# The second layer's gate projections by seven block products for eight, and an attention table in a buffer of its own

## Chip, cores and metric

The kernel runs on one core of one Trainium2 chip. The metric is the time of one execution in device microseconds, the median of several runs.

## The reference

Two layers of a trunk over 1024 latent tokens and 256 context tokens, width 1024, float32. In each layer four token mixers (chunked gMLP, Fourier, convolution, neighbourhood attention) give branch rows a, b, cc, d of width 256, which are merged through gates:

```python
za, zb, zcv, zq, zk, zv, zg = jnp.split(h @ w_in[l], SPLITS, axis=-1)
...
def merge_branches(a, b, cc, d, zg, w_a, w_b, w_c, w_d, w_o):
    ga, gb, gc, gd = jnp.split(jax.nn.sigmoid(zg), N_BRANCH, axis=-1)
    m = ga * (a @ w_a) + gb * (b @ w_b) + gc * (cc @ w_c) + gd * (d @ w_d)
    return m @ w_o
```

zg, the gate projection, is 1024 tokens by 4 x 1024 columns. A mixture of experts follows the merge. In the second layer context tokens are needed only as keys and values, so that its gates cover the 1024 latent tokens alone.

## The kernel before

Every operand of a large matmul is kept as two parts. `split` makes them: ACT copies the operand to a float32r tile (hi, L422), and DVE subtracts that from the operand (lo, L423). `mm3` (L427 to L429) multiplies hi by hi, hi by lo and lo by hi into one PSUM sum: three matmuls for one k-tile of 128, each with a moving operand of 512 tokens.

`gates` (L1092) runs once for each layer, transposed: output columns on partitions, tokens along the row. Its loops are over four branches i and, inside, eight column blocks d of 128. For each (i, d), `proj_T` multiplies the weight block by the tokens' normed rows (tiles hTh and hTl, eight k-tiles, two halves of 512 tokens): 48 matmuls into one PSUM tile A of 128x1024. ACT takes the sigmoid from A into g (L1158). Then 12 matmuls multiply the branch rows (bh, bl, two k-tiles) by the branch weights (wbh, wbl) into another A, and DVE multiplies that by g and adds it to mT (L1173, or L1175 and L1176), which holds all of m in SBUF.

Weights come by SP's queue through the class `Split`, which splits them in order and ahead. Branch rows are stored in DRAM (`self.br`) and loaded by POOL's queue in `load` (L1132), twice for each branch, when the branch changes; ACT and DVE split them.

PSUM tiles come from pools that hand out tile A (1024 wide, two banks) and X and T (512 wide). SBUF tiles come from pools with a number of buffers for each name; a new tile of a name waits for the last use of the one whose place it takes. Each engine runs its instructions in the order of the program.

`merge_out` (L1194) multiplies m by w_out, token tile by token tile. While the first weights are split, eight plain matmuls (L1219) of the first k-tile from mT fill TensorE; `out_m` (L1354) splits m for a token tile. POOL's queue loads the router's weights (L1206), the norm's gains and rows of modulation (L1340) at its start.

In the attention, POOL makes a bias table `Bu` of a unit's kind (L282) that DVE adds to the scores (L317, the start of the softmax); two pairs of `Bu` buffers alternate, both taken from the pool that is opened for the attention. `Vw` holds windows of the values, loaded by 16 DMAs on SP's queue (L264).

Of the kernel before, what the change touches and what calls it, by code (L numbers as in the profile page):

```python
# [18 lines left out]
D = 1024  # L19
SEQ = 1024  # L20
CTX = 256
# [3 lines left out]
KD = D // 128  # L25
# [77 lines left out]
class Split:  # L103
# [62 lines left out]
    def ready(self, n):  # L166

        self.prefetch()
        self.split(self.i + n)
# [13 lines left out]
class Attention:  # L183
# [10 lines left out]
    def __init__(self, K, p, V, Vc):  # L194
        self.K, self.V, self.Vc, self.nc = K, V, Vc, K.nc
        nc, l, I = K.nc, K.l, K.I
        self.rt = p
        self.rope = p.tile([128, 2, SEQ], F32, name="rope")
        nc.sync.dma_start(self.rope, I["c_rope"].rearrange("a p t -> p a t"))
        cm = p.tile([128, 120], F32, name="cm")  # L200
        nc.sync.dma_start(cm, I["c_att"])
        self.load_bias(0)

        self.ca = p.tile([128, 2, 3, 12, 32], BF16, name="ca")
        rows, cols = cm[:, :24].rearrange("p (g k) -> p g k", g=2), cm[:, 24:].rearrange("p (c x) -> p c x", c=3)
# [6 lines left out]
        self.H = [{}, {}]  # L212

    def load_bias(self, hp):

# [34 lines left out]

    def buffers(self):
        nc, w = self.nc, self.work
        self.B = [[w.tile([128, self.ALL], F32, name=f"Bu{i}{h}") for h in range(2)] for i in range(2)]
        for b in self.B:
            for h in range(2):
                nc.gpsimd.memset(b[h][:, self.KEYS:], 0.0)
        self.tables, self.nt = {}, 0
# [120 lines left out]
    def heads(self, vqk, prep):  # L378

        K, N = self.K, len(self.units)  # L380
        K.sides.append(prep)
        self.table(0)
        U = {0: self.scores(0)}
        for n in range(N + 2):
            u, p = U.get(n), U.get(n - 1)
            self.table(n + 1)

            if p:
                self.trans(p, 0)
                self.trans_copy(p, 0)  # L390
            if u:
                self.soft(u, 0)
            if p:
                self.norm(p, 1)
            if n - 2 in U:
                self.values(U[n - 2], vqk)
            if p:
                for i in (1, 2):
                    self.trans(p, i)
                self.trans_copy(p, 1)  # L400
            if u:
                self.soft(u, 1)
                self.norm(u, 0)
            if p:
                self.trans_copy(p, 2)
            if n + 1 < N:
                if self.units[n + 1][0] and not self.units[n][0]:
                    K.finish(prep)
                U[n + 1] = self.scores(n + 1)
            K.tick()  # L410


class Trunk:
# [43 lines left out]
    def run(self, stop=None):  # L457
        ctx, tc, nc, I = self.ctx, self.tc, self.nc, self.I
# [4 lines left out]
        dp = ctx.enter_context(tc.tile_pool(name="dr", bufs=1, space=DRAM))  # L463
# [9 lines left out]
        self.modrow = dp.tile([DEPTH, 2, 48, 128], F32, name="modrow")  # L473
        self.x1 = [dp.tile([SEQ, D], F32, name=f"x1_{l}") for l in range(DEPTH)]
        self.xc1 = dp.tile([CTX, D], F32, name="xc1")
        self.h2 = [dp.tile([SEQ, HEXT], F32, name=f"h2_{l}") for l in range(DEPTH)]
        self.hc2 = dp.tile([CTX, HEXT], F32, name="hc2")

# [114 lines left out]
    def layer(self, l, stop):  # L593
        tc, nc = self.tc, self.nc
        last = l == DEPTH - 1
        self.l, self.last = l, last
        self.ncols = SEQ if last else SEQ + CTX
        def pool(cx, name, side="left"):
            return cx.enter_context(tc.tile_pool(name=name, bufs=1, reuse_waits="tile", side=side))
        with ExitStack() as ex:  # L600
            if l == 0:
                self.sil = pool(ex, "first").tile([128, KD, 32], F32, name="sil")
                nc.vector.memset(self.sil, 0.0)
            with ExitStack() as self.mctx:
                self.graw = pool(self.mctx, "graw", "right")
                with tc.tile_pool(name="hT", bufs=1, reuse_waits="tile") as hp:

                    self.hTh, self.hTl = ([[hp.tile([128, w], F32R, name=f"hT{part}{a}_{k}") for k in range(KD)]
                                           for a, w in enumerate((512, 512, CTX))] for part in "hl")
                    self.mixers()  # L610
                    if stop == ("mix", l):
                        return False
                    mpool = pool(self.mctx, "mT", "right")
                    self.mT = mpool.tile([128, KD, self.ncols], F32, name="mT")
                    with tc.tile_pool(name="gates", bufs=1, reuse_waits="tile") as gp:
                        self.gates(gp)
                self.merge_out(ex)
            if stop == ("out", l):
                return False
            self.experts(ex)  # L620
        return stop != ("ffn", l)
# [569 lines left out]
                self.mod_fin(*fin.pop())  # L1191


    def merge_out(self, ex):  # L1194
        nc, l, I, last, tc = self.nc, self.l, self.I, self.last, self.tc
        with tc.tile_pool(name="wo", bufs=1, reuse_waits="tile") as p:
# [5 lines left out]
            X = {}  # L1202
# [13 lines left out]
            raw0 = self.gst.get()[0]  # L1216
            for t in order[:2]:
                for h in range(2):
                    nc.tensor.matmul(X[t]["A"][h], self.mT[:, 0, t * 128:(t + 1) * 128], raw0[:, 0, h * 512:h * 512 + 512],  # L1219
                                     start=True, stop=False)  # L1220
            self.out_m(X[order[0]])
            for k in range(1, KD):
                raw = self.gst.get()[0]
# [130 lines left out]
    def out_m(self, S):  # L1354
        t, p = S["t"], self.op
        S["mh"] = p.tile([128, KD, 128], F32R, name="mh", bufs=2)
        S["ml"] = p.tile([128, KD, 128], F32R, name="ml", bufs=2)
        self.split(S["mh"], S["ml"], self.mT[:, :, t * 128:(t + 1) * 128])

    def out_mm(self, S, wh, wl, hs, ks):  # L1360
        A = S.setdefault("A", [])
# [584 lines left out]
```

## Time and profile before

| | us |
|---|---|
| median of 3 runs (3535.12 to 3535.59) | 3535.59 |
| profiled execution | 3546.22 |
| its span | 3544.1 |
| stretch 2385 to 2790, second layer's gates | 405.0 |
| attention of layer 2, about 2279 to 2360 | 81 |

The span is the part of the profiled execution that the trace covers. Busy times, waits and clocks below are of that one execution; a granted clock of 1.00 is 2.4 GHz and 0.50 is 1.2 GHz. An idle time in brackets behind a row is that before it, with the instruction that released it.

### The profile page before, as it was taken

The page shows a single profiled execution, that of the slowest core. Times are in us where ns is not written, and L with a number is a line of the kernel's source. Part 1 is how long each engine was busy: PE and PEld are TensorE (multiplying, and loading weights), DVE is VectorE, ACT ScalarE, POOL GpSimd, SP SyncE. Part 2 cuts the span into 40 slices and gives each one's busy share as a digit, 9 for nine tenths or more (in the row PEclk, how much of TensorE's full clock was granted, in tenths as well). Part 3 has the DMA queues.
Part 4 walks back from the last instruction along what each step waited for, and adds up shares of the span by engine and source line. Part 5 has one row for each costly group of instructions (what it writes and reads, how often), then busy time and mean ns, then how long its engine had stood idle before and what let it go on. Part 6 is the DMA issues. An engine that isn't in the chain of part 4 may idle for free.

```text
span 3544.1 us, 46796 instructions
## 1 busy us (share of the span) xinstructions
PE 3374.3 (95%) x18735; PEld 2608.8 (74%) x18735; DVE 2122.5 (60%) x2822; ACT 1544.4 (44%) x2053; POOL 807.0 (23%) x688
## 2 busy tenths in 40 slices
PE   7999999999999699999999899999999988999997
PEld 5997688888877466666666588778888766888885
DVE  5866512232245577777777677552223458999998
ACT  4114511111125365665655531451112255777776
POOL 3104100000005613332331110320000053444430
PEclk9999999999999799999999999999999998999999
DMA  6113333333133778887888811322121368999995
GB/s 213 37 56 76 92 90 104 98 97 111 54 120 134 254 258 294 289 280 284 290 287 285 293 49 50 81 76 65 42 66 55 113 244 308 389 381 389 382 388 203
DMA packets 287404, 653.54 MB, mean 184 GB/s; under 512 B 32255, under 2 KB 127349, under 8 KB 287186
## 3 DMA queue, kind: packets, MB, share of 16 engines
q1 hardware_dynamic: 258962, 551.35, 43.7%
q0 software_dynamic: 28048, 99.12, 9.4%
q8 instruction: 147, 2.41, 0.3%
q14 instruction: 71, 0.58, 0.0%
q10 hardware_dynamic: 176, 0.08, 0.0%
HBM read 594.60 MB, written 51.70 MB: 182 GB/s over the span
## 4 chain that ended last, share of the span: by engine, by line
PE 51%; issue 6%; DVE 6%; DMA 3%; ACT 2%; POOL 1%; SPq 0%; POOLq 0%; DVEq 0%; ACTq 0%
PE A L427 14%; PE A L428 14%; PE A L429 14%; PE X L1723 4%; DVE wlo L423 1%; DMA x<-y,idx 1%; PE T L1826 1%; DVE cacc L933 1%; ACT whi L422 1%; PE T L1779 1%; DVE y L1841 1%; POOL oh L1734 0%; DMA wraw<-in_w_down_e_dram 0%; DMA xe<-h,idx 0%; DVE xo L1387 0%
## 5 line engine op out<-in xcount | busy, mean ns | idle before, releaser
L423 DVE TENSOR_TENSOR wlo<-wraw,whi 128x1024 fp32r<-128x1024 f32 x864 | 1020.2, 1226 | 443.9 <-ACT whi L422 438.3
L422 ACT ACTIVATE whi<-wraw 128x1024 fp32r<-128x1024 f32 x864 | 865.2, 1052 | 291.5 <-PE A L429 262.7
L427 PE MATMUL A<-hTh,whi 128*128 128x512 f32 x1280 | 511.7, 400 | 1.9 <-ACT whi L422 1.9
L428 PE MATMUL A<-hTl,whi 128*128 128x512 f32 x1280 | 499.9, 391 | 3.8 <-POOL hTl L669 2.1
L429 PE MATMUL A<-hTh,wlo 128*128 128x512 f32 x1280 | 500.1, 391 | 2.7 <-DVE wlo L423 2.7
L427 PE MATMUL A<-whi,xh 128*128 128x512 f32 x1024 | 419.2, 409 | 1.4 <-ACT whi L422 1.4
L428 PE MATMUL A<-wlo,xh 128*128 128x512 f32 x1024 | 405.3, 396 | 2.0 <-DVE wlo L423 1.0
L429 PE MATMUL A<-whi,xl 128*128 128x512 f32 x1024 | 403.2, 394 | 0.6 <-DVE xl L423 0.6
L1158 ACT ACTIVATE g<-A 128x1024 f32<-128x1024 f32 x64 | 65.7, 1027 | 728.4 <-PE A L429 630.1
L427 PEld LDWEIGHTS A<-hTh,whi 128*128 128x128 f32 x1280 | 241.1, 188 | 61.6 <-issue 12.4
L429 PEld LDWEIGHTS A<-hTh,wlo 128*128 128x128 f32 x1280 | 240.7, 188 | 55.5 <-DVE wlo L423 4.5
L428 PEld LDWEIGHTS A<-hTl,whi 128*128 128x128 f32 x1280 | 241.2, 188 | 53.3 <-POOL hTl L669 2.9
L1734 POOL TENSOR_SCALAR oh<-cs,slot 128x128 bf16<-128x128 f32 x232 | 276.8, 1209 | 1.0
L1842 POOL DMA_INDIRECT x<-y,idx x31 | 50.5, 1630 | 847.4 <-DVE y L1841 847.4
L427 PEld LDWEIGHTS A<-whi,xh 128*128 128x128 f32 x1024 | 194.2, 190 | 66.5 <-issue 15.1
L1175 DVE TENSOR_TENSOR g<-A,g 128x1024 f32<-128x1024 f32 x46 | 56.3, 1224 | 288.9 <-PE A L429 288.9
L428 PEld LDWEIGHTS A<-wlo,xh 128*128 128x128 f32 x1024 | 194.6, 190 | 45.6 <-DVE wlo L423 10.0
L429 PEld LDWEIGHTS A<-whi,xl 128*128 128x128 f32 x1024 | 194.1, 190 | 43.5 <-DVE xl L423 1.3
L427 PE MATMUL A<-whi,gh 128*128 128x512 f32 x512 | 207.9, 406 | 0.2 <-ACT gh L422 0.2
L428 PE MATMUL A<-wlo,gh 128*128 128x512 f32 x512 | 201.8, 394 | 0.9 <-DVE wlo L423 0.9
L429 PE MATMUL A<-whi,gl 128*128 128x512 f32 x512 | 201.0, 393 | 0.0
L933 DVE SCALAR_TENSOR_TENSOR cacc<-cy,par,cacc 128x1310 f32<-128x1310 f32 (+1 forms) x120 | 190.9, 1591 | 3.4
(406 smaller groups left out, 5894.6 us busy)
## 6 DMA issues: line engine op xcount, KB each, us to landing
wraw<-in_w_up_e_dram SPq DMA_DIRECT2D x126, 1024.0 KB, 6.9
wraw<-in_w_gate_e_dram SPq DMA_DIRECT2D x125, 1024.0 KB, 8.3
wraw<-in_w_down_e_dram SPq DMA_DIRECT2D x122, 1024.0 KB, 7.9
wraw<-in_w_in_dram SPq DMA_DIRECT2D x96, 512.0 KB, 4.3
wraw<-in_w_mod_dram SPq DMA_DIRECT2D x68, 512.0 KB, 4.4
wraw<-in_w_mod_dram SPq DMA_DIRECT2D x14, 1024.0 KB, 8.2
h<-h POOLq DMA_DIRECT2D x16, 520.0 KB, 3.7
wraw<-in_w_out_dram SPq DMA_DIRECT2D x16, 512.0 KB, 4.7
```

The costliest lines, as they stand in the source:

```text
L422: nc.scalar.activation(hi, src, AF.Copy)
L423: (eng or nc.vector).tensor_tensor(lo, src, hi.bitcast(F32), op=OP.subtract)
L427: mm(out, lh, rh, start=start, stop=False)
L428: mm(out, lh, rl, start=False, stop=False)
L429: mm(out, ll, rh, start=False, stop=stop)
L933: nc.vector.scalar_tensor_tensor(acc[:, j, :], y[:, w:w + n_out], wc, acc[:, j, :], op0=OP.mult, op1=OP.add)
L1158: nc.scalar.activation(g[:, :SEQ], A, AF.Sigmoid)
L1175: nc.vector.tensor_tensor(g[:, s], o, g[:, s], op=OP.mult)
L1723: nc.tensor.matmul(X[32 * g:32 * g + 32, :], x, raw[:, kk, h * 512:h * 512 + 512], start=(q == 0), stop=(q == 3))
L1734: eng.tensor_scalar(S["oh"][:, t, :], iota, self.slot[:, t, e:e + 1], None, op0=OP.is_equal)
L1779: nc.tensor.transpose(T[:, k * 128:(k + 1) * 128], S["xe"][:, (4 * a + k) * 128:(4 * a + k + 1) * 128], self.ident)
L1842: nc.gpsimd.indirect_dma_start(out=self.x1[l][:, :], out_offset=bass.IndirectOffsetOnAxis(ap=S["idx"][:, :1], axis=0), in_=y, in_offset=No ...
```

## The change

The first layer's `gates` stays. The second layer runs `gates_last`. It has 16 groups: column pairs d = 0, 2, 4, 6 outermost and the four branches inside. A group covers two column blocks, two token halves and two halves of k. Groups 0 and 1 do the eight block products as before; the other 14 do seven, from sums of the blocks:

- On the tokens' side T1, T2, T3 (differences of halves of the normed rows) are made once, by a generator that runs in group 0; T4 is made at the start of group 2 and overwrites the tiles of the block "12" there is no more use for.
- On the weights' side POOL makes s1 to s4 (128x512) for each group (L1283 and L1287 of the change), and the seven operands are split 512 wide.
- The products run in the order x11, s2, x12, x22, s3, s1, s4. They go to halves q0 to q3 of two tiles A. Their results are combined 512 wide: ACT copies q0 into c11 (L1360), DVE adds (u2 L1362, c11 L1365, then c21, c22, c12), and sigmoids follow.
- The branch rows are loaded anew in each group, through a tile `br` with one buffer, in `bh_load`, which stands after the second product; the branch products follow the seven.
- m is kept as `mp` for one column pair. It is stored to DRAM (`mD`) by POOL's queue after a pair's last branch, and read back in `m_load` by SP's queue, a token tile at a time, for the merge; POOL copies the last pair (`m_last`).
- Context rows of the normed tokens have a pool of their own, freed before the gates.
- Attention: the first pair of `Bu` buffers is taken with the attention's constants, so that its memsets and the first table are issued there; `Vw` windows are loaded with the block of columns outermost.

```diff
 # Attention.__init__, buffers and heads
+        self.tables, self.nt, self.B = {}, 0, []
+        self.bias_room(p)
         units = [(g, cb) for g in range(2) for cb in range(4)] + ([] if K.last else [(2, t) for t in range(2)])
         self.units = [(hp, g, cb) for hp in range(2) for g, cb in units]
         self.H = [{}, {}]
+        self.table(0)
...
-        for r in range(4):
-            for cb in range(4):
+        for cb in range(4):
+            for r in range(4):
...
+        self.bias_room(w)
...
-        self.table(0)
         U = {0: self.scores(0)}
 # gates_last
+            for k in range(4):
+                t = mp.tile([128, 1024], F32, name="mr", bufs=2)
+                y21, t2 = t[:, :512], t[:, 512:]
+                for y, n in ((y21, "21"), (t2, "T2")):
+                    h, lo = Y[n][k]
+                    nc.vector.tensor_tensor(y, h.bitcast(F32), lo.bitcast(F32), op=OP.add)
+                nc.gpsimd.tensor_tensor(y21, y21, t2, op=OP.subtract)
+                self.split(*Y["T4"][k], y21)
+                yield 3
...
+                    for o, a, b, op in ((s1, x(1, 0), x(1, 1), OP.add), (s2, s1, x(0, 0), OP.subtract),
+                                        (s3, x(0, 0), x(1, 0), OP.subtract)):
+                        nc.gpsimd.tensor_tensor(o, a, b, op=op)
...
+            A = [self.ps.tile([128, 1024], F32, name="A") for _ in range(2)]
+            q = [A[j // 2][:, halves[j % 2]] for j in range(4)]
+            g = [p.tile([128, 1024], F32, name="g", bufs=2) for _ in range(2)]
+            def bh_load():
+                S["b"] = []
+                for k in range(2):
+                    b = p.tile([128, 1024], F32, name="br", bufs=1)
+                    nc.gpsimd.dma_start(b, self.br[i][k * 128:(k + 1) * 128, :1024])
+                    bh, bl = p.tile([128, 1024], F32R, name=f"bh{k}"), p.tile([128, 1024], F32R, name=f"bl{k}")
+                    S["b"].append((b, bh, bl))
+                    self.split(bh, bl, b)
+                wh, wl = p.tile([128, 2, 256], F32R, name="wbh"), p.tile([128, 2, 256], F32R, name="wbl")
+                self.split(wh, wl, S["wb"])
...
+                if gi == 2:
+                    Y["T4"] = Y["12"]
+                    self.finish(side)
...
+                plan = [("x11", 0, "11"), ("s2", 1, "T2"), ("x12", 0, "21"), ("x22", 2, "T4"), ("s3", 1, "T3"),
+                        ("s1", 3, "T1"), ("s4", 0, "22")]
+                for j, (w, o, y) in enumerate(plan):
+                    ready(n + 3)
+                    product(q[o], S[w], y, True, True)
+                    n += 1
+                    if w == "x11":
+                        AC(c11, q[0], AF.Copy)
+                    elif w == "s2":
+                        nc.vector.tensor_tensor(u2, q[1], c11, op=add)
+                        bh_load()
+                    elif w == "x12":
+                        nc.vector.tensor_tensor(c11, q[0], c11, op=add)
+                        AC(c11, c11, AF.Sigmoid)
+                    elif w == "s3":
+                        nc.vector.tensor_tensor(c21, q[1], u2, op=add)
...
+            if i == 3 and d < KD - 2:
+                for j in range(2):
+                    nc.gpsimd.dma_start(self.mD[(d + j) * 128:(d + j + 1) * 128, :], m[:, j, :])
```

DVE, in the gates before, at a branch change: the lo parts of a weight block (wlo) and of branch weights (wbl), and the two steps into mT.

```order
L1176 TENSOR_TENSOR mT<-mT,g 128x1024 [waits DVE_49]
L423 TENSOR_TENSOR wlo<-wraw,whi 128x1024 [waits DMAHW7_49,Activation_49]
L423 TENSOR_TENSOR wbl<-wraw,wbh 128x1024 [waits DMAHW5_49,Activation_49]
L1175 TENSOR_TENSOR g<-A,g 128x1024 [waits PE_49,Activation_49]
L1176 TENSOR_TENSOR mT<-mT,g 128x1024 [waits DVE_49]
L423 TENSOR_TENSOR wlo<-wraw,whi 128x1024 [waits DMAHW0_49,Activation_49]
```

In the change, in the middle of a seven-product group: the lo of x22, u2, the lo of both branch rows and of the branch weights, the lo of s3, and the add of x12's result into c11.

```order
L428 TENSOR_TENSOR wlo<-wraw,whi 128x512 [waits DMAHW4_49,Activation_49]
L1362 TENSOR_TENSOR u_19766<-A,g 128x512 [waits PE_49]
L428 TENSOR_TENSOR bl_19800<-br,bh_19799 128x1024 [waits DMASW6_49,Activation_49]
L428 TENSOR_TENSOR bl_19806<-br,bh_19805 128x1024 [waits DMASW7_49,Activation_49]
L428 TENSOR_TENSOR wbl<-wraw,wbh 128x512 [waits DMAHW5_49,Activation_49]
L428 TENSOR_TENSOR wlo<-s_19679,whi 128x512 [waits Activation_49]
L1365 TENSOR_TENSOR g<-A,g 128x512 [waits DVE_49,PE_49]
```

The add into c11 (L1365), which reads the PSUM half that x12 filled, now stands behind the work on two loaded branch rows and waits, as they do, in DVE's order.

POOL's queue in the gates before: the branch loads, and the loads of the merge.

```order
L1132 DMA g<-br_68 128x1024 [waits DMASW1_49,DVE_49]
L1132 DMA g<-br_69 128x1024 [waits DMASW4_49,DMASW2_49,DMASW5_49,DVE_49,Activation_49]
L1132 DMA g<-br_69 128x1024 [waits DMASW3_49,DVE_49,Activation_49]
L590 DMA modrow<-modr 48x2x128 [waits DMASW6_49,DVE_49]
L1132 DMA g<-br_70 128x1024 [waits DMASW4_49,DMASW7_49,DVE_49,Activation_49]
L1132 DMA g<-br_70 128x1024 [waits DMASW5_49,DVE_49,Activation_49]
```

In the change: the two branch loads of a group, the sums s1 to s4, the stores of m and the next group's loads.

```order
L1327 DMA br<-br_70 128x1024 [waits DMASW5_49]
L1327 DMA br<-br_70 128x1024 [waits DMASW6_49,DVE_49]
L1283 TENSOR_TENSOR s_19870<-wraw 128x512 [waits DMAHW7_49,DVE_49]
L1283 TENSOR_TENSOR s_19871<-s_19870,wraw 128x512 [waits DMAHW6_49,DVE_49,Pool_49]
L1283 TENSOR_TENSOR s_19872<-wraw 128x512
L1287 TENSOR_TENSOR s_19871<-wraw,s_19871 128x512 [waits DVE_49]
L1399 DMA mD<-mp 128x1024 [waits DVE_49] x2
L1327 DMA br<-br_67 128x1024 [waits DMASW7_49]
L1327 DMA br<-br_67 128x1024 [waits DMASW2_49,DVE_49]
```

The second of each pair of loads now waits for DVE, which must have read the one buffer, and a pair stands in every group.

TensorE in the change, at the border of the products s2 (on T2) and x12 (on the block 21).

```order
L433 MATMUL A<-T2l_19102,whi 128x512
L434 MATMUL A<-T2h_19101,wlo 128x512
L432 MATMUL A<-hTh_4_16181,whi 128x512 [waits DVE_49]
L433 MATMUL A<-hTl_4_16197,whi 128x512
L434 MATMUL A<-hTh_4_16181,wlo 128x512
```

In the gates before, ACT and DVE read a tile A when both of its halves are complete; here x12's first matmul waits for DVE, since it overwrites a half of the tile whose other half DVE's u2 reads.

ACT in the change: the copy of c11, the hi part of x22, of both branch rows and the branch weights, of s3, and the sigmoid of c11.

```order
L427 ACTIVATE whi<-wraw 128x512 [waits PE_49,Activation_49]
L1360 ACTIVATE g<-A 128x512 [waits DVE_49,PE_49]
L427 ACTIVATE whi<-wraw 128x512 [waits DMAHW4_49,Activation_49]
L427 ACTIVATE bh_19799<-br 128x1024 [waits DMASW6_49]
L427 ACTIVATE bh_19805<-br 128x1024 [waits DMASW7_49]
L427 ACTIVATE wbh<-wraw 128x512 [waits DMAHW5_49]
L427 ACTIVATE whi<-s_19679 128x512 [waits Activation_49,Pool_49]
L1366 ACTIVATE g<-g 128x512 [waits DVE_49]
```

The hi parts of what the next products need now stand behind those of the branch rows, each of which waits for its load.

## Rows read from the trace of the kernel before

**Rows 1.** The page: span; busy time of TensorE and its share.

```profile
span 3544.1 us, 46796 instructions
...
PE 3374.3 (95%) x18735; PEld 2608.8 (74%) x18735; DVE 2122.5 (60%) x2822; ACT 1544.4 (44%) x2053; POOL 807.0 (23%) x688
```

**Rows 2.** Windows, second layer's gates: busy time by engine, granted clock, DMA share, GB/s.

```profile
2385.00:2790.00 405.00, 405.00 (x1789) 335.29 (x1789) 113.11 (x96) 71.66 (x72) 6.86 (x12) 1.00 0.19 55
```

**Rows 3.** Groups of instructions, 2385 to 2790 us: ACT's split of the branch rows.

```profile
L422 ACT ACTIVATE bh<-g 128x1024 fp32r<-128x1024 f32 x6 | 6.3, 1052 | 13.8 <-DMA g<-br 13.8
```

**Rows 4.** Timeline of TensorE, last gate matmul of a column block: start, duration.

```profile
2466.87 0.39 PE L429 MATMUL A<-hTh,wlo 128*128 128x512 f32 x1
```

**Rows 5.** Timeline of ACT at two branch changes.

```profile
2467.30 1.03 ACT L1158 ACTIVATE g<-A 128x1024 f32<-128x1024 f32 x1 [11.63 <-PE A L429]
...
2475.34 1.06 ACT L422 ACTIVATE bh<-g 128x1024 fp32r<-128x1024 f32 x1 [3.53 <-DMA g<-br]
...
2585.75 1.06 ACT L422 ACTIVATE bh<-g 128x1024 fp32r<-128x1024 f32 x1 [5.16 <-DMA g<-br]
```

**Rows 6.** Groups of instructions by form, whole span: operations 512 wide.

```profile
L423 DVE TENSOR_TENSOR xl<-T,xh 128x512 fp32r<-128x512 f32 x64 | 43.4, 679 | 13.4 <-ACT xh L422 13.4
...
L351 ACT ACTIVATE PT<-T 128x512 f32<-128x512 f32 x64 | 38.2, 597 | 47.0 <-PE T L343 46.9
L1387 DVE TENSOR_TENSOR xo<-xo,xi 128x512 f32<-128x512 f32 x36 | 37.7, 1058 | 1.0
...
L1377 DVE TENSOR_TENSOR xo<-A,bc 128x512 f32<-128x512 f32 x36 | 24.3, 686 | 32.6 <-PE A L429 32.6
...
L247 POOL TENSOR_TENSOR k<-k,rt 128x512 f32<-128x512 f32 x8 | 10.5, 1310 | 1.0 <-issue 0.7
```

**Rows 7.** Timeline of DVE: the add ahead of a branch load.

```profile
2580.15 1.22 DVE L1176 TENSOR_TENSOR mT<-mT,g 128x1024 f32<-128x1024 f32 x1
```

**Rows 8.** Timeline of POOL: two issues of branch loads.

```profile
2471.61 0.53 POOL L1132 DMA_DIRECT2D g<-br  x1 [13.07 <-DVE mT L1173]
...
2581.89 0.53 POOL L1132 DMA_DIRECT2D g<-br  x1 [13.07 <-issue]
```

**Rows 9.** Tile br, second layer's gates: from issue to landing.

```profile
DMA to landing us min/median/max: 3.1/3.8/6.2
```

**Rows 10.** Timeline of TensorE at the merge's start.

```profile
2796.49 3.60 PE L1219 MATMUL A<-wraw,mT 128*128 128x512 f32 x8
```

**Rows 11.** Timeline of DVE and TensorE at the start of the second layer's attention.

```profile
2281.84 0.82 DVE L317 CUSTOM_DVE_ANT_0 P<-A,Bu 128x640 f32<-128x640 f32 x1 [4.41 <-POOL Bu L282]
...
2282.73 1.87 PE L295 MATMUL A<-k,qr 64*128 64x384 f32 x3 [2.61 <-DVE sm L317]
```

**Rows 12.** Waits of TensorE in the attention of layer 2, then of layer 1.

```profile
PE A L295 <- DVE sm L317: 4.3, 2, 2.6
...
PE X L367 <- DMA Vw<-V: 2.0, 1, 2.0
```

**Rows 13.** Windows of 2.5 us after idleness of TensorE; columns as in rows 2.

```profile
1082.50:1085.00 2.50, 0.64 (x3) 0.19 (x1) 1.13 (x2) 1.71 (x5) 0.00 (x0) 1.00 0.99 308
1085.00:1087.50 2.50, 2.12 (x13) 1.86 (x14) 2.11 (x8) 0.30 (x1) 0.00 (x0) 1.00 0.21 85
1115.00:1117.50 2.50, 1.05 (x17) 0.58 (x18) 1.12 (x1) 1.90 (x4) 2.42 (x2) 1.00 0.27 110
1117.50:1120.00 2.50, 2.50 (x9) 1.93 (x9) 2.47 (x3) 0.21 (x1) 2.50 (x1) 0.65 0.00 0
1120.00:1122.50 2.50, 2.50 (x12) 2.10 (x11) 1.64 (x4) 0.72 (x2) 1.85 (x3) 0.67 0.03 7
2282.50:2285.00 2.50, 2.27 (x6) 1.56 (x7) 2.31 (x8) 1.79 (x4) 1.93 (x3) 0.50 0.92 205
2285.00:2287.50 2.50, 2.50 (x10) 1.51 (x8) 2.46 (x6) 0.33 (x1) 1.93 (x2) 0.50 0.96 204
2287.50:2290.00 2.50, 2.50 (x13) 1.49 (x12) 1.79 (x4) 2.50 (x7) 2.42 (x3) 0.70 0.96 198
```

More of the change, by code (lines that the diff above doesn't have):

```diff
@@ L212, in __init__, with bias_room @@
         self.H = [{}, {}]
+        self.table(0)
+    def bias_room(self, p):
+        b = [p.tile([128, self.ALL], F32, name=f"Bu{len(self.B)}{h}") for h in range(2)]
+        for h in range(2):
+            self.nc.gpsimd.memset(b[h][:, self.KEYS:], 0.0)
+        self.B.append(b)
     def load_bias(self, hp):
@@ L252, in buffers @@
         nc, w = self.nc, self.work
[L253 to L257, printed above, removed]
         self.Vw = w.tile([128, 4, 4, W], F32, name="Vw")
         Vr = self.V.rearrange("p (a two) w -> p a two w", two=2)
-        for r in range(4):
-            for cb in range(4):
+        for cb in range(4):
+            for r in range(4):
                 at = r % 2 * 64 + self.FROM[cb]
                 nc.sync.dma_start(self.Vw[32 * r:32 * r + 32, cb], Vr[at:at + 32, :, r // 2, :])
+        self.bias_room(w)
     def table(self, n):
@@ L475, in run @@
         self.xc1 = dp.tile([CTX, D], F32, name="xc1")
+        self.mD = dp.tile([D, SEQ], F32, name="mD")
         self.h2 = [dp.tile([SEQ, HEXT], F32, name=f"h2_{l}") for l in range(DEPTH)]
@@ L606, in layer @@
                 with tc.tile_pool(name="hT", bufs=1, reuse_waits="tile") as hp:
[L608 to L616, printed above, removed]
+                    self.hTh, self.hTl = ([[hp.tile([128, 512], F32R, name=f"hT{part}{a}_{k}") for k in range(KD)]
+                                           for a in range(2)] for part in "hl")
+                    with ExitStack() as hx:
+                        hc = pool(hx, "hTc")
+                        for part, x in (("h", self.hTh), ("l", self.hTl)):
+                            x.append([hc.tile([128, CTX], F32R, name=f"hT{part}2_{k}") for k in range(KD)])
+                        self.mixers()
+                        if stop == ("mix", l):
+                            return False
+                        mpool = pool(self.mctx, "mT", "right")
+                        self.mpool = mpool
+                        if not last:
+                            self.mT = mpool.tile([128, KD, self.ncols], F32, name="mT")
+                            with tc.tile_pool(name="gates", bufs=1, reuse_waits="tile") as gp:
+                                self.gates(gp)
+                    if last:
+                        with tc.tile_pool(name="gates", bufs=1, reuse_waits="tile") as gp:
+                            self.gates_last(gp, mpool)
                 self.merge_out(ex)
@@ L1194, in merge_out, with m_load, m_last @@
+    def m_load(self, t, p, early=False):
+        r = self.mr[t] = p.tile([128, 1024], F32, name="mr", bufs=2).rearrange("p (k c) -> p k c", c=128)
+        self.nc.sync.dma_start(r[:, :6, :], self.mD[:768, t * 128:(t + 1) * 128].rearrange("(k p) c -> p k c", p=128))
+        if not early:
+            self.m_last(t)
+    def m_last(self, t):
+        self.nc.gpsimd.tensor_copy(self.mr[t][:, 6:, :], self.mp[:, :, t * 128:(t + 1) * 128])
     def merge_out(self, ex):
@@ L1218, in merge_out @@
                 for h in range(2):
-                    nc.tensor.matmul(X[t]["A"][h], self.mT[:, 0, t * 128:(t + 1) * 128], raw0[:, 0, h * 512:h * 512 + 512],
-                                     start=True, stop=False)
+                    m0 = self.mr[t][:, 0, :] if last else self.mT[:, 0, t * 128:(t + 1) * 128]
+                    nc.tensor.matmul(X[t]["A"][h], m0, raw0[:, 0, h * 512:h * 512 + 512], start=True, stop=False)
             self.out_m(X[order[0]])
@@ L1357, in out_m @@
         S["ml"] = p.tile([128, KD, 128], F32R, name="ml", bufs=2)
-        self.split(S["mh"], S["ml"], self.mT[:, :, t * 128:(t + 1) * 128])
+        if self.last:
+            self.split(S["mh"], S["ml"], self.mr[t])
+            if t + 2 < 8:
+                self.m_load(t + 2, self.mpool)
+        else:
+            self.split(S["mh"], S["ml"], self.mT[:, :, t * 128:(t + 1) * 128])
     def out_mm(self, S, wh, wl, hs, ks):
```

132 lines of the change are left out of this document (added).

## Prediction

> **What bounds the kernel now.** First the page: TensorE is busy 95% of a span of 3544.1 us [rows 1]. Then the windows, for the stretch that is rewritten: the second layer's gates, where TensorE is busy in all of the 405.00 us between 2385 and 2790, at a granted clock of 1.00, with DVE at 113.11 us and ACT at 71.66 us [rows 2]. There TensorE alone sets the time; 1789 recorded matmuls in 405.00 us are one in 0.226 us (0.227 below). So a matmul less is a gain, and a wait more is a loss of its full length. Last, how the loop keeps TensorE fed: DVE and ACT always have a branch product or a gate product of slack, and the only engine that waits for a transfer is ACT, 13.8 us for its branch rows, which TensorE doesn't feel [rows 3].
>
> **What is removed.** 14 groups of 12 matmuls: 168 x 0.227 = **-38.1 us**. Branch products stay at 24 a group.
>
> **What is added: waits of TensorE inside each of the 14 seven-product groups.** A product is now 12 matmuls, 2.72 us of issue, and its result is read 512 wide as soon as it is complete. Two products in a row go to halves of one PSUM tile A, and the change waits for the reader of the one half before it writes the other. I time a group from the start of x11, with handoffs from the present loop: the last gate matmul starts at 2466.87 and takes 0.39 [rows 4], and ACT reads at 2467.30 [rows 5]; so 0.17 us pass from the end of issue to data and 0.04 more to ACT (I take 0.1 to DVE).
>
> (1) s2 waits for ACT's copy of c11. The nearest row is the PSUM copy 128x512 of ACT, 597 ns [rows 6]: 2.72 + 0.17 + 0.05 + 0.60 + 0.03 = 3.57, idle **0.85**.
>
> (2) x12 waits for u2 on DVE, whose nearest row is an add from PSUM 128x512, 686 ns [rows 6]: 3.57 + 2.72 + 0.17 + 0.10 + 0.69 + 0.04 = 7.29, idle **1.0**. x12 and x22 then run to 7.29 + 5.44 = 12.73.
>
> (3) s3 overwrites the half next to x12's and so waits for the add into c11. On DVE that add stands behind u2, bl of both branch rows, wbl and the lo part of s3. Both branch rows come through one buffer: POOL issues the second load only when DVE has made the first bl. So: u2 ends at 7.26, bl (1.22, as the add of 128x1024 [rows 7]) at 8.4. From the end of a DVE instruction to the POOL issue that waits for it 0.52 pass (2580.15 + 1.22 = 2581.37; issue at 2581.89), and from that issue to ACT's split of what it loads 3.73 (2471.61 to 2475.34) [rows 5, 7, 8]; the second issue of rows 8 gives 3.86. bh starts at 12.7 and takes 1.06; bl follows to 15.0, wbl and s3's lo (each 128x512, 679 ns [rows 6]) to 16.2, the add to 16.85. s3 starts at 16.9: idle **4.15**. Bounds: transfers of these rows land 3.1 to 6.2 us after issue, 3.8 in the median [rows 9]. At 3.1 without handoffs s3 is idle 2.9, at 6.2 it is 6.5. I take the median.
>
> The other products hide theirs: s4 waits for the sum of x12 (two products earlier), the next x11 for c21 (24 branch matmuls, 5.4 us, lie between). Sum of a group 6.0, x14 = **+84** (66 to 117). DVE has some 17 us of work in a group of 24.5 us of matmuls, so it is late here by order, not by load.
>
> **Added once, or a few times.** At the first such group T4 is made from four k-tiles one after the other: two DVE adds (0.7 each), a POOL subtract (1.31, the 128x512 row on POOL [rows 6]), ACT 0.60, DVE 0.68: with handoffs 4.1 each, 16.4 in all, and ACT's c11 copy stands behind it. Less the 2.7 of x11 already under way: **+15** (8 to 16). In group 0 the branch rows are loaded in the middle and the branch product waits for wbl: +3.5 (2 to 8). After each of the three stores of m, POOL's queue holds the next branch load behind an issue that waits for DVE's last add: +6 in all (0 to 9). Merge: the first filler matmuls now read rows that POOL completes after the last add (a copy of 128x256, and the queue's router loads behind it); today the eight fillers (3.60 us from 2796.49) start without a gap [rows 10]: +3 (0 to 6).
>
> **Attention.** The first score product of layer 2 waits 2.61 us for DVE's softmax start, which waits for POOL's table [rows 11]; in layer 2 such waits sum to 4.3 us, and layer 1 loses 2.0 us on the V windows [rows 12]. Tables built earlier and windows loaded in order of use can give back 6.3 at most, and a clock stretch of 3.2 (below): I take **-4** (0 to -9).
>
> **The clock.** TensorE's row at 2282.73 follows 2.61 us of idleness [rows 11]; the granted clock is then 0.50 in two slices of 2.5 us from 2282.5 and 0.70 in the third, that is 5.0 + 1.5 = 6.5 us at 1.2 GHz in which half is lost, 3.2 us [rows 13]. At 1115 an idle 1.45 us is followed by 0.65 and 0.67, 3.4 us at half and 1.7 lost; at 1082.5 1.86 us of idleness is followed by none. So the 4.15 before s3 likely costs a fall in each group, the waits of 0.85 and 1.0 do not by themselves, and what a fall slows (s3, s1, s4) nothing hides. Two us x 16 (14 groups, T4 and one more) = **+32** (0 to 54). The Trainium skill, page "TensorE: Matmul & The Clock Gate", section "HAM oscillation — how this bites in real kernels", says that a loop whose TensorE waits in each of its tiles starts every tile on the lowered clock and pays each time; the trace agrees at 2280 and not at 1082.5. With none of the groups spared and the larger price, 14 x 3.2 = 45, the sum would be 13 higher.
>
> **Sum.** -38 + 84 + 15 + 3.5 + 6 + 3 - 4 + 32 = +101. The profiled execution takes 3546.2 us (3544.1 of span, 2.1 around it), so 3647; the runs' median, 3535.6, lies 10.6 below it, so **3637**.
>
> **Rivals.**
> (a) The waits come as worked out, but the clock holds at 2.4 GHz. For it: the 1.86 us at 1082.5 with no fall. Against: 4.15 is longer than any idleness in these rows. 3637 - 32 = 3605.
> (b) All is longer: landings at 6.2 (+33 over 14 groups), or the DVE adds beside POOL's four s sums, as the add between SBUF tiles takes 1058 ns where that from PSUM takes 686 [rows 6] (+0.37 on two of them in each group, +10), and falls of 3.2. 3660 to 3700, middle 3680. Against: POOL's sums mostly lie outside the chain u2 to c11.
> (c) The second branch load is hidden (a landing before x22 ends), and with it the clock fall: -38 + 26 (waits 1 and 2) + 15 + 3.5 + 3 - 4 = +5, 3541. It needs a landing 4.15 us earlier than rows 8 show, that is no transfer at all; the only way is that the load doesn't wait for bl.
> (d) The other side: the halves of A don't hold TensorE back. The mechanism is that a product is written beside a half still being read, so none of (1) to (3) is paid: -38 + 15 + 3.5 + 3 - 4 = -21, some 3515. It decides from a wait below about 1.4 us in a group (-21 + 14 x 1.4 = 0), where 6.0 is forecast. Against: each product's first matmul stands behind a semaphore of the reader, as the pairs of rows in the order show.
>
> **How the numbers follow.** Forecast 0.52, (a) 0.23, (b) 0.16, (c) 0.05, (d) 0.04. The predicted time is the forecast's, 3637; its own range is 3615 to 3655. The range to give holds (a) with a margin for its bounds (at the lower wait of s3, 3605 - 18 = 3587) and the lower half of (b): 3585 to 3690. What is about as large as this measurement can tell from none is 0.2%, 7 us: (c) falls within it or just beside it, so same 0.04, faster 0.05 ((d) and a little of (c)), slower 0.91.
>
> **What would show it.** In the windows of the second gates the clock falls below 1.00 and TensorE is idle some 100 us. Its waits name ACT's copy of c11 (0.85 each, 14 times), DVE's u2 (1.0) and DVE's sum into c11 (about 4.2); ACT's bh waits for the branch DMA once in each group; one gap of 15 us lies at group 2. If the wait of s3 is under 2 us, step (3) is wrong; if the clock stays at 1.00 through these gaps, the last term is. The attention's term is right if TensorE no longer waits for the softmax start in layer 2's first unit. The prediction is wrong altogether if the seven-product groups last below 24.5 + 1.4 = 25.9 us.

## The result, and the profile after

The changed kernel takes 3650.66 us (median of 6 runs, 3648.42 to 3657.45), the kernel before 3535.59 in the same 6 rounds (3534.84 to 3539.47): ratio 1.0327, 95% interval 1.0314 to 1.0340. It is 115 us slower; 3637 were forecast.

The page of the changed kernel, span and busy times [rows 1]: TensorE's busy time is about what it was, with 168 matmuls fewer, and the span 102 us longer.

```profile
span 3646.6 us, 47270 instructions
...
PE 3376.2 (93%) x18567; PEld 2590.7 (71%) x18567; DVE 2287.4 (63%) x3116; ACT 1616.0 (44%) x2203; POOL 928.9 (25%) x798
```

The windows of the second gates from the first seven-product group on, columns as in rows 2: TensorE is busy in 381.61 of 463 us, at a granted clock of 0.91 on average, where it was busy in all of the time at 1.00.

```profile
2425.00:2888.00 463.00, 381.61 (x1502) 299.61 (x1503) 237.42 (x336) 126.62 (x194) 91.72 (x88) 0.91 0.27 82
```

How long the second gates last is read from two timelines of TensorE, their first matmul and the first of the merge's fillers. The last row here is the one wait of the merge to which we come below.

```profile
2343.69 0.50 PE L432 MATMUL A<-hTh,whi 128*128 128x512 f32 x1
```

```profile
2888.15 3.60 PE L1444 MATMUL A<-wraw,mr 128*128 128x512 f32 x8
...
2904.26 0.80 PE L432 MATMUL A<-woh,mh 128*128 128x512 f32 x1 [4.99 <-ACT woh L427]
```

2888.15 - 2343.69 = 544.5 us, against 436.4 before (to the fillers' 2796.49 [rows 10], from this row):

```profile
2360.04 0.50 PE L427 MATMUL A<-hTh,whi 128*128 128x512 f32 x1 [0.71 <-ACT whi L422]
```

The waits of TensorE in this stretch (line, what released it; total us, times, longest):

```profile
PE A L432 <- DVE g L1365: 58.5, 14, 6.9
PE A L432 <- ACT g L1360: 24.4, 14, 15.4
PE A L432 <- DVE u L1362: 11.0, 14, 0.8
PE X L432 <- ACT wbh L427: 5.4, 1, 5.4
PE A L434 <- DVE wlo L428: 1.9, 2, 1.2
PE X L434 <- DVE wbl L428: 0.7, 1, 0.7
```

They are the three waits that were forecast, 14 times each, and small ones of groups 0 and 1 (the last three lines). Rows of TensorE's timeline at the ends of these waits, groups 2 and 3; the second row is the first matmul of group 3's x11:

```profile
2427.98 0.79 PE L432 MATMUL A<-T2h,whi 128*128 128x512 f32 x1 [15.40 <-ACT g L1360]
...
2458.82 0.39 PE L432 MATMUL A<-hTh,whi 128*128 128x512 f32 x1
...
2462.39 0.50 PE L432 MATMUL A<-T2h,whi 128*128 128x512 f32 x1 [0.69 <-ACT g L1360]
...
2466.19 0.50 PE L432 MATMUL A<-hTh,whi 128*128 128x512 f32 x1 [0.78 <-DVE u L1362]
...
2475.24 0.77 PE L432 MATMUL A<-T3h,whi 128*128 128x512 f32 x1 [3.29 <-DVE g L1365]
...
2476.23 0.63 PE L434 MATMUL A<-T3h,wlo 128*128 128x512 f32 x1
2476.65 0.63 PE L432 MATMUL A<-T3h,whi 128*128 128x512 f32 x1
```

In group 2 TensorE stands 15.40 us at the c11 copy, behind T4. In group 3 it waits 0.69 for the copy, 0.78 for u2, and then 3.29 for the sum into c11; in all later groups the first two are the same, and the third lies between 3.2 and 6.9. An interruption costs more than the idle time in brackets: from s2's first matmul to x12's 3.80 us pass, of which 12 matmuls take 2.72 and the idle time 0.78, so 0.30 more are lost. What that last wait consists of is read in the timelines of DVE, POOL and ACT of group 3. DVE first:

```profile
2465.44 0.69 DVE L1362 TENSOR_TENSOR u<-A,g 128x512 f32<-128x512 f32 x1 [1.86 <-PE A L434]
2466.05 1.22 DVE L428 TENSOR_TENSOR bl<-br,bh 128x1024 fp32r<-128x1024 f32 x1
2472.06 1.23 DVE L428 TENSOR_TENSOR bl<-br,bh 128x1024 fp32r<-128x1024 f32 x1 [4.79 <-ACT bh L427]
2473.20 0.68 DVE L428 TENSOR_TENSOR wbl<-wraw,wbh 128x512 fp32r<-128x512 f32 x1
2473.80 0.68 DVE L428 TENSOR_TENSOR wlo<-s,whi 128x512 fp32r<-128x512 f32 x1
2474.41 0.68 DVE L1365 TENSOR_TENSOR g<-A,g 128x512 f32<-128x512 f32 x1
```

POOL, the two issues of the group's branch loads. The second row names a weight load as its releaser, but what it waits for in POOL's order is DVE, and in all 14 groups it starts 0.29 to 0.31 us behind the end of the first bl:

```profile
2456.40 0.56 POOL L1327 DMA_DIRECT2D br<-br  x1
2467.57 0.54 POOL L1327 DMA_DIRECT2D br<-br  x1 [10.61 <-DMA wraw<-in_w_in_dram]
```

ACT, the c11 copy and the second branch row's hi part:

```profile
2461.73 0.60 ACT L1360 ACTIVATE g<-A 128x512 f32<-128x512 f32 x1 [4.86 <-PE A L434]
...
2470.97 1.06 ACT L427 ACTIVATE bh<-br 128x1024 fp32r<-128x1024 f32 x1 [7.17 <-DMA br<-br]
```

Read together: DVE ends the first bl at 2467.27, POOL issues the second load at 2467.57, ACT can split its rows at 2470.97, 3.40 us later, and has waited 7.17 for them. DVE has nothing to do for 4.79 us, since the next in its order is the bl of that row; then come wbl, the lo of s3 and, last, the add (2474.41) that TensorE is waiting for. s3 starts at 2475.24.

The clock at this wait: windows of 20 us, each from some 3 us ahead of s3's start, columns as in rows 2, of groups 3, 4, 6 and 9:

```profile
2472.00:2492.00 20.00, 16.77 (x68) 13.76 (x69) 14.30 (x21) 5.99 (x11) 6.05 (x5) 0.91 0.08 25
2507.00:2527.00 20.00, 16.60 (x62) 13.54 (x63) 11.46 (x18) 6.16 (x11) 5.97 (x5) 0.78 0.11 34
2571.00:2591.00 20.00, 16.57 (x61) 13.18 (x60) 11.54 (x18) 6.61 (x11) 5.97 (x5) 0.83 0.08 23
2671.00:2691.00 20.00, 16.53 (x73) 13.44 (x72) 15.49 (x22) 6.45 (x11) 6.47 (x5) 1.00 0.18 57
```

0.91, 0.78, 0.83 and 1.00. A mean of 0.91 over 20 us is 20 x 0.09 / 0.5 = 3.6 us at 1.2 GHz, 0.83 is 6.8 and 0.78 is 8.8. Of the 14 groups 6 have 0.91, 5 have 0.83, 2 have 0.78 and one has 1.00, after a wait of 3.47 us like the others'. A part of that time can lie in the wait itself, where it costs nothing. What the clock costs is seen in the matmuls: the last two rows of TensorE above start 0.42 us apart, where 0.227 is usual. In the whole of the second gates 160 matmuls start over 0.25 us behind the one before with no wait between (the restart behind a wait, up to 0.37, is left out), and lose some 32 us in all: about 1.5 to 3.0 behind each wait of s3, none in group 9.

### The profile page after: what moved, and what is told of

It reads as the page before. It is cut to its first block, busy times and chain, and to the rows that moved or that the text cites. A ratio compares the mean times of both kernels' runs of the same rounds, so it can differ in the third digit from the quotient of the medians.

```text
span 3646.6 us, 47270 instructions
## 1 busy us (share of the span) xinstructions
PE 3376.2 (93%) x18567; PEld 2590.7 (71%) x18567; DVE 2287.4 (63%) x3116; ACT 1616.0 (44%) x2203; POOL 928.9 (25%) x798
## 5 line engine op out<-in xcount | busy, mean ns | idle before, releaser
L428 DVE TENSOR_TENSOR wlo<-wraw,whi 128x1024 fp32r<-128x1024 f32 (+1 forms) x882 | 1023.6, 1205 | 470.1 <-ACT whi L427 465.1
L427 ACT ACTIVATE whi<-wraw 128x1024 fp32r<-128x1024 f32 (+1 forms) x882 | 862.4, 1027 | 292.9 <-PE A L434 264.5
L432 PE MATMUL A<-hTh,whi 128*128 128x512 f32 x1056 | 426.0, 403 | 11.3 <-DVE u L1362 11.0
L434 PE MATMUL A<-hTh,wlo 128*128 128x512 f32 x1056 | 412.9, 391 | 3.6 <-DVE wlo L428 3.6
L433 PE MATMUL A<-hTl,whi 128*128 128x512 f32 x1056 | 412.6, 391 | 3.8 <-POOL hTl L684 2.1
L432 PEld LDWEIGHTS A<-hTh,whi 128*128 128x128 f32 x1056 | 199.1, 189 | 67.9 <-DVE u L1362 17.2
L434 PEld LDWEIGHTS A<-hTh,wlo 128*128 128x128 f32 x1056 | 198.4, 188 | 48.3 <-DVE wlo L428 5.7
L433 PEld LDWEIGHTS A<-hTl,whi 128*128 128x128 f32 x1056 | 199.1, 189 | 44.1 <-POOL hTl L684 3.0
L1173 ACT ACTIVATE g<-A 128x1024 f32<-128x1024 f32 x32 | 32.9, 1029 | 398.8 <-PE A L434 325.6
L433 PE MATMUL A<-wlo,hTh 128*128 128x256 f32 x592 | 168.8, 285 | 10.1 <-DVE wlo L428 10.1
```

The source lines that it names most:

```text
L427: nc.scalar.activation(hi, src, AF.Copy)
L428: (eng or nc.vector).tensor_tensor(lo, src, hi.bitcast(F32), op=OP.subtract)
L432: mm(out, lh, rh, start=start, stop=False)
L433: mm(out, lh, rl, start=False, stop=False)
L434: mm(out, ll, rh, start=False, stop=stop)
L1173: nc.scalar.activation(g[:, :SEQ], A, AF.Sigmoid)
```

## The experiments

Each time is a median; the medians of the kernel before, run beside each, lay between 3535.6 and 3539.9, so that a difference in us between two experiments is good to a few us. A ratio is that of the runs of the two kernels, with its 95% interval.

**The kernel before once more (c_before).**

> The kernel before, once more, for a second trace. Theory: the first profiled execution was 10.6 us above its median because of waits in the merge of layer 1 and at the start of its experts, and not in the gates; this one has a span near 3534 and second gates of 436 us again. Rival: the 10.6 lie in the gates or are spread evenly, and the span is 3544 again.

One run, span 3536.4 us. The first gate matmul of layer 2 and the first filler of the merge in its trace:

```profile
2351.52 0.50 PE L427 MATMUL A<-hTh,whi 128*128 128x512 f32 x1 [0.71 <-ACT whi L422]
```

```profile
2787.96 3.60 PE L1219 MATMUL A<-wraw,mT 128*128 128x512 f32 x8
```

The gates last 436.4 us again, and what follows them 748.4 (747.6 in the first trace); they begin 8.5 us earlier than the 2360.04 of the first trace. So what makes the first trace 7.7 us longer than this one lies ahead of the second gates, and the sum of the prediction's terms may be put on the median, as it was. (That these us lie in the merge of layer 1 and its experts is not shown.)

**Two buffers for the branch rows (e1_br2).**

```diff
-                    b = p.tile([128, 1024], F32, name="br", bufs=1)
+                    b = p.tile([128, 1024], F32, name="br", bufs=2)
```

> The changed kernel with two buffers for br instead of one. Theory (the second branch load waits for DVE and holds up s3 through DVE's order; each of these waits brings a clock fall): the 58.5 us of waits for the sum into c11 vanish, and with them most of the lost clock, some 35: about 3557 us (3545 to 3575); the waits for the c11 copy and for u2 stay at about 9 + 15 and 11. Rival 1 (DVE's order itself: four lo parts ahead of that sum, however early the rows land): s3 still waits about 2 us in each group, 3610 to 3625. Rival 2 (the clock does not fall because of these gaps): only the 58, 3592.

3565.32 us, ratio 1.0069 (1.0052 to 1.0087): 85 us less from one number. The waits:

```profile
PE A L432 <- ACT g L1360: 23.9, 14, 14.9
PE A L432 <- DVE u L1362: 11.0, 14, 0.8
PE A L432 <- DVE g L1365: 8.5, 3, 3.1
```

Of the 58.5 us of waits for the sum into c11 8.5 are left, in 3 groups of 14; the other two are as they were. The theory holds, and rival 1 falls: with the rows there, DVE's order delays nothing. In the trace the second gates last 465.5 us (2345.26 to 2810.77), 79 less: 55 of waits (50 there, 5 in group 0), and 22 of clock, as 51 matmuls start late, with 10 us lost, where it was 160 with 32. So rival 2 falls.

**The products on alternating tiles (e2_tiles).**

```diff
-                plan = [("x11", 0, "11"), ("s2", 1, "T2"), ("x12", 0, "21"), ("x22", 2, "T4"), ("s3", 1, "T3"),
-                        ("s1", 3, "T1"), ("s4", 0, "22")]
+                plan = [("x11", 0, "11"), ("s2", 2, "T2"), ("x12", 1, "21"), ("x22", 3, "T4"), ("s3", 0, "T3"),
+                        ("s1", 2, "T1"), ("s4", 1, "22")]
```

The sums read the halves accordingly.

> The changed kernel with the products spread over the two tiles A in turn (x11, s2, x12, x22, s3, s1, s4 into halves 0, 2, 1, 3, 0, 2, 1), so that no product follows another into the same tile while its first half is read. Theory: the waits for the c11 copy (0.7 a group) and for u2 (0.8) vanish, but the branch rows' chain starts only that much earlier and ends as late for TensorE, so s3 waits about 1.4 longer: 3645 to 3655, no change. Rival (the three waits add up): 20 us less, 3630.

3638.17 us, ratio 1.0282 (1.0265 to 1.0299), between theory and rival: 12 us less than the changed kernel by the medians, 16 by the ratios, 7 by the spans of the traces. The waits:

```profile
PE A L432 <- DVE g L1365: 82.4, 14, 9.2
PE A L432 <- ACT g L1360: 12.6, 1, 12.6
```

The waits for u2 and, but for T4's, for the copy are gone, and that for the sum into c11 is 82.4 us instead of 58.5: 95.0 in all where it was 93.9. So the waits did what the theory said; the chain through the branch load began earlier and TensorE waited at its end. Yet the second gates last 536.8 us, 7.7 less than in the changed kernel. Of all interruptions there are 27 fewer, each worth the 0.30 us found above: 8 us, less the 1.1 us by which the waits grew, are 7 of these.

**Both (e3_both).**

> Both edits together. Theory: no wait left in groups 3 to 15, only the 15 us of T4 and the 7 us of groups 0 and 1, and a clock of nearly 1.00: 20 less than with two buffers alone, about 3537 us (3525 to 3550), about the kernel before. Rival: DVE, with 17 us of work in a group and its order, becomes the next to be waited for, and the time stays above 3560.

3544.19 us, ratio 1.0015 (1.0005 to 1.0024), as the theory has it. The waits that are left:

```profile
PE A L432 <- DVE g L1365: 16.3, 4, 5.8
PE A L432 <- ACT g L1360: 12.3, 1, 12.3
```

The second edit, the tiles, now gives 21 us, since little is left that waits behind it: what an edit is worth depended on the other. DVE is no bound. Left are T4's wait and 16.3 us in 4 groups; the long ones stand in groups 4, 8 and 12.

**The idle time ahead of s3 filled with work (e4_fill).**

```diff
+                    if w == "s3":
+                        X = self.ps.tile([128, 512], F32, name="X")
+                        for _ in range(18):
+                            nc.tensor.matmul(X, S["x22"][0][:, 0, :], Y["T4"][0][0], start=True, stop=True)
                     product(q[o], S[w], y, True, True)
```

> The changed kernel with 18 matmuls added ahead of each s3, of x22's first block by T4 into a tile X that nobody reads: some 4.1 us of work in the place of the idle time before s3, 252 matmuls or 57 us in all. Theory (idle TensorE is what the clock falls follow, one fall of 2 to 3 us in each group after the wait for the sum into c11): the wait is filled, the clock stays at 1.00 behind it, and the kernel is faster by 25 to 40 us with more work: 3610 to 3626. Rival (the falls follow anything else, as the group's rhythm or the sum of load): 0 to 5 us, 3645 to 3651, or slower, if the added matmuls delay s3.

3627.40 us, ratio 1.0250 (1.0235 to 1.0266): 252 matmuls more, and 23 us less. Windows of the stretch 2425 to 2888, and the waits:

```profile
2425.00:2888.00 463.00, 426.61 (x1795) 339.45 (x1796) 251.39 (x345) 133.78 (x201) 101.51 (x97) 0.98 0.31 93
```

```profile
PE A L432 <- ACT g L1364: 24.3, 14, 15.4
PE A L432 <- DVE u L1366: 11.0, 14, 0.8
PE A L432 <- DVE g L1369: 9.7, 4, 3.3
```

The same stretch has a clock of 0.98 where it was 0.91. The gates last 526.3 us (2341.3 to 2867.6), 18.2 less; 57.2 of work were added and 50.1 of waits went (48.8 of them at s3), so 25 us were given back, nearly all by the clock: 40 matmuls start late, with 9 us lost, where it was 160 with 32. The time itself, 23 us less, is just short of the theory's 25 to 40, and far from the rival's 0 to 5.

**The attention's part alone (e5_attn),** on the kernel before.

> The kernel before with the attention's part of the change alone (first table and memsets with the constants, windows of V by column block first). Theory: -3 us, 3.5 of it in layer 1 (the 2.0 us wait for the windows is gone) and nothing in layer 2, where TensorE's wait for the softmax start goes from 4.3 to 2.9 us but the waits for P grow by 1.5; ratio 0.998 to 1.000. Rival (the 15 us by which the changed kernel's first trace is ahead when the second gates begin are its doing): 0.996.

3534.49 us against 3538.70, ratio 0.9991 (0.9982 to 1.0000): 3 us by the ratio and 4 by the medians, as forecast, with an interval from 0 to 6: just at the edge of what these runs can tell.

**The stores of m behind the branch loads (e6_store),** with the two edits above.

```diff
                         bh_load()
+                        if i == 0:
+                            for j2 in range(2):
+                                nc.gpsimd.dma_start(self.mD[(d - 2 + j2) * 128:(d - 1 + j2) * 128, :], m[:, j2, :])
...
-            if i == 3 and d < KD - 2:
-                for j in range(2):
-                    nc.gpsimd.dma_start(self.mD[(d + j) * 128:(d + j + 1) * 128, :], m[:, j, :])
```

> Two buffers for br and the spread tiles, and the stores of m issued behind the next group's branch loads instead of ahead of them. Theory (in groups 4, 8 and 12 POOL's queue holds both branch loads behind a store that waits for the last add): of the 16.3 us of waits for the sum into c11 that were left some 14 go, and three clock falls: 3544 - 14 - 7 = 3523 (3516 to 3530). Rival (these waits come from DVE's load in these groups): 3540 to 3546.

3524.59 us, ratio 0.9955 (0.9939 to 0.9970). The wait for the sum into c11 is gone from TensorE's list; the longest left in the gates is T4's, 12.2 us. So the waits of groups 4, 8 and 12 came from POOL's queue.

**T4 earlier, and the merge's loads on another queue (e7_best).** T4 is made in pairs of k-tiles (four adds, two subtracts, then two splits), from the third product of group 1 on, and `m_load` issues by POOL unless early.

> As the run before, and T4 made in pairs of k-tiles from the third product of group 1 on, behind which 10.9 us of matmuls are left, and the token tiles of m for the merge loaded by POOL's queue instead of SP's. Theory: the wait of 12.3 us at group 2 goes to 0 to 3, with one or two clock falls (-12 to -15), and the merge no longer waits 5 us for w_out, whose loads stood on SP behind a load that waits for DVE (-6): 3523 - 13 - 6 = 3504 (3497 to 3515), faster than both kernels by about 1%. Rival 1 (T4's chain in the order of ACT and DVE holds up the splits for group 2 for as long as it held up group 2 itself): 3517. Rival 2 (the merge waits for HBM's share and not for the queue): 3510.

3518.17 us, ratio 0.9936 (0.9923 to 0.9950), 14 us more than expected. 5.5 us of a wait at group 2 were left, and the merge still waits for w_out:

```profile
2773.86 0.80 PE L432 MATMUL A<-woh,mh 128*128 128x512 f32 x1 [3.86 <-ACT woh L427]
```

So SP's queue was at most the smaller part of what held w_out up (4.99 us before), and both of the rivals hold in part.

**T4 earlier still, and the last pair of m by ACT (e8_best2).**

```diff
-                for j, w in enumerate(("x11", "x12", "x21", "x22")):
+                for j, w in enumerate(("x11", "x21", "x12", "x22")):
...
-        self.nc.gpsimd.tensor_copy(self.mr[t][:, 6:, :], self.mp[:, :, t * 128:(t + 1) * 128])
+        self.nc.scalar.activation(self.mr[t][:, 6:, :], self.mp[:, :, t * 128:(t + 1) * 128], AF.Copy)
```

> As the run e7_best, with the four products of groups 0 and 1 in the order x11, x21, x12, x22, so that T4's chain starts after the second and has 16.3 us of matmuls behind it instead of 10.9, and with the last pair of m copied by ACT instead of POOL, so that POOL issues the loads of the router and of the modulation rows before the merge and not beside w_out's. Theory: the 5.5 us wait at group 2 and a clock fall go (-7), and part of the merge's 3.9 us and its fall (-3 to -6): 3518 - 11 = 3507 (3502 to 3513). Rival (w_out is late because the token tiles of m, rows of 512 bytes, are loaded at the same time): the merge keeps its wait, 3511.

3519.68 us, ratio 0.9944 (0.9930 to 0.9957): nothing gained. The waits of TensorE in the merge:

```profile
PE X L1659 <- ACT h2T L1651: 6.4, 4, 3.0
PE A L432 <- ACT woh L427: 1.9, 2, 1.2
```

w_out's wait went from 3.9 to 1.9 us, which points to the loads of router and modulation rows beside it as the larger part of the rest; but ACT's copies for later token tiles put 6.4 us of waits for h2T in its place (2.0 before), and the other order made group 1 wait 3.25 us for a sigmoid.

**Eight products in the change's loop (e9_eight).** Every group does the eight products; nothing is made for the seven.

> The changed loop with eight products in all 16 groups, no T and no s sums; two buffers for br, stores of m behind the branch loads. It has the change's order, its loads and its merge, and 168 matmuls more than e6_store. Theory (new order and merge cost only the merge's 8 us and the first group's wait, the attention gives 3 to 4 back): 3538.7 + 8 + 2 - 4 = 3545 (3538 to 3550); against e6_store's 3524.6 the seven products are then worth some 20 of their 38 us, the rest being T4's wait with its clock. Rival (the order itself costs more, in 512-wide splits and reloaded branch rows): over 3555.

3539.30 us, ratio 0.9999 (0.9990 to 1.0009). Its second gates last 436.6 us, as in the kernel before, so order, reloaded rows and 512-wide splits cost nothing there, and the rival falls; that the merge costs what the attention gives back is not shown by itself. Against it the seven products of e6_store are worth 14.7 of their 38 us; 12.2 of the difference is T4's wait, and some 5 are lost to a lower clock.

**The last version (e10_best3).** The other order in group 1 alone, ACT's copy for the first two token tiles alone.

> As e7_best, with the other order of the products in group 1 alone (in group 0 it had made the next group wait 3.25 us for a sigmoid on A), and with ACT copying the last pair of m for the first two token tiles alone, POOL for the others (ACT's copies for the later ones had made TensorE wait 4 to 5 us more for h2T). Theory: both gains of e8_best2 without its two new waits: 3518 - 5.5 and a clock fall of 3 at group 2, - 3 in the merge: 3507 (3502 to 3512). Rival (what the waits gave back is taken elsewhere, as in e8_best2): 3516 to 3520.

3507.65 us, ratio 0.9912 (0.9898 to 0.9926): 30 us faster than the kernel before and 143 faster than the changed one. The number is the expected one, the reason is so in part: the merge no longer waits for w_out, but in group 1 a product waits as long as group 2 had,

```profile
2390.93 0.79 PE L432 MATMUL A<-hTh,whi 128*128 128x512 f32 x1 [5.70 <-ACT g L1358]
```

for a sigmoid that stands on ACT behind the splits of the T tiles. T4's term was moved, not won, so an estimate from this wait is that some 5 us more are to be had here.

## Why the prediction was right, point by point

| term | forecast | measured | read from |
|---|---|---|---|
| 168 matmuls | -38.1 | -38.1 | same pitch |
| wait for the c11 copy | +12 | +9.0 | idle times, 24.4 - 15.4 |
| wait for u2 | +14 | +11.0 | idle times |
| wait for the sum into c11 | +58 | +48.6 | 58.5 less the next row |
| the same behind stores of m | +6 | +9.9 | 6.88, 6.62 and 6.78 where 11 others have 3.2 to 4.1 |
| T4 | +15 | +15.4 | idle time |
| groups 0 and 1 | +3.5 | +8.0 | 5.4 + 1.9 + 0.7 |
| clock | +32 | +32 | late matmuls |
| restarts | in the waits | +12 | 544.5 - 1752 x 0.227 - 101.9 - 32.4 |
| merge | +3 | +7.8 | see below |
| attention | -4 | -4 | e5_attn |
| sum | +101 | +113 | the runs: +115 |

**The waits** were where the order and the rows put them. The forecast counted from start to start, so the restarts belong to its waits: counted so, the waits of group 3 are 0.85, 1.08 and 3.6 us where 0.85, 1.0 and 4.15 were forecast. Step (3) had the transfer as 3.7 to 3.9 us and the issue behind DVE as 0.5; in group 3 they measured 3.40 and 0.30 (in all 14 groups 3.3 to 4.2, mean 3.6, and 0.3), which is most of that difference. Too low were the stores of m and group 0, whose 5.4 us come from the same single buffer (0.3 with two). e1_br2 shows that the single buffer makes this wait, and e6_store that the stores of m add to it.

**The clock** was the term with the widest bounds (0 to 54) and came out as forecast, and so did the 2 us of a fall (1.5 to 3.0). Its mechanism was tested by e4_fill: with work in the place of idleness 25 us came back, nearly all of them clock. Rival (a), the clock at 2.4 GHz throughout, is out by the windows. The rows from which the 2 us came are weaker than the prediction reads them: its 1.45 and 1.86 us are idle shares of slices, while the longest single idle time of TensorE in the timeline is 1.00 us ahead of the fall at 1117.5 and 2.24 at 1082.5, where none follows. So a price that came out right was partly luck. That each group pays, as the page "TensorE: Matmul & The Clock Gate" of the Trainium skill ("HAM oscillation — how this bites in real kernels") says of loops with a wait in each tile, agrees with 13 of the 14, and not with group 9, whose clock held behind 3.47 us of idleness.

**The merge** was mis-sized. Measured as the router's first matmul, it moved by 99.5 us (2810.1 to 2909.6) where the fillers moved by 91.7. The forecast had fillers that start later; they start without a gap. What it priced too low is, as far as the runs tell, the group of loads behind the POOL copy. Before, POOL issued the rows of modulation 10 us ahead of the fillers, and TensorE had no wait for a split of w_out's hi part:

```profile
2786.17 1.61 POOL L1340 DMA_DIRECT2D bc<-modrow  x3 [93.25 <-issue]
```

The timelines of SP and of POOL at the merge's start in the changed kernel:

```profile
2891.34 0.37 SPq L1410 DMA_DIRECT2D mr<-mD  x1
2892.41 0.33 SPq L135 DMA_DIRECT2D wraw<-in_w_out_dram  x1
```

```profile
2888.50 0.74 POOL L1415 COPY mr<-mp 128x256 f32<-128x256 f32 x2 [24.87 <-DVE mp L1396]
2889.19 0.91 POOL L1430 DMA_DIRECT2D wr<-in_w_router_dram  x1
...
2890.62 1.61 POOL L1564 DMA_DIRECT2D bc<-modrow  x3
```

Router, modulation rows and token tiles of m are loaded between 2889 and 2894, with w_out's fourth piece issued at 2892.41, and TensorE waits 4.99 us for its split. e7_best took the token tiles off SP's queue and the wait stayed; with the router's and modulation's loads issued earlier it fell to 1.9 us (e8_best2) and to nothing (e10_best3).

**The attention** gave the 4 us, but not in the way that was forecast. The prediction's own sign was that TensorE no longer waits for the softmax start in layer 2's first unit. It still does, for 1.01 us instead of 2.61, and in layer 2 what these waits lose (4.3 to 2.9 us) the waits for P gain (1.7 to 3.2):

```profile
2265.69 1.33 PE L301 MATMUL A<-k,qr 64*128 64x384 f32 x3 [1.01 <-DVE sm L323]
```

```profile
PE T L349 <- DVE P L335: 3.2, 4, 1.4
PE A L301 <- DVE sm L323: 2.9, 2, 1.9
```

Only layer 1's wait of 2.0 us for the V windows is gone. That the number fits is luck.

**The rivals.** (b) had landings of 6.2 us, DVE adds of 1058 ns and falls of 3.2 us; the second load was read 3.3 to 4.2 us after its issue, u2 and the sum into c11 took DVE 0.69 and 0.68, and no fall behind a wait of s3 cost over 3.0. (c), the load hidden, is the kernel e1_br2 in effect. (d), halves that don't hold TensorE back, is out by the list of waits: all three stand in it, 14 times each. e2_tiles takes only the first two away (s3 is still written beside x12's half and waits for its reader), and alone gained little.

## What to carry to other kernels

Before work is taken from the engine that sets the time, write down what the shorter steps wait for in each engine's order: 2.7 us saved in a group were paid for with 4.9 us of idle time, all made by a buffer too few and by an order that puts products into the tile that is still being read. A chain of waits ends in one place, so an edit at its start (the tiles) is worth little (12 us) until that at its end (the buffer) is made, and both together gave 106 us. Where TensorE has to wait in each round of a loop, count the restart and the clock behind the wait as well; here the two cost 12 and 32 us on top of 102 of waits.

## What the runs showed of the hardware that was not expected

Adding 57 us of matmuls that nobody reads made the kernel 23 us faster: they stood in the place of 50 us of waits, and the granted clock in that stretch rose from 0.91 to 0.98, which gave back about 24. And at waits of almost the same length, 3.2 to 4.1 us, the clock was low for anything from 0 to 6.8 us, so that a fall cannot be priced from the wait alone.
